# More background steps in the paired projections, the retention gate as a background item, and the gate scan behind three query norms

## The chip, the cores and the metric

One core of a Trainium2 chip. TensorE (PE) multiplies, VectorE (DVE) and ScalarE (ACT) work on elements, GpSimd (POOL) does some element work and issues DMAs, SyncE (SP) issues the other DMAs. The metric is the device time of one execution in microseconds; the median of several runs counts.

## The reference, cut to what matters

Two layers on a sequence of 512 tokens with model width 1024. In each layer the normalized and modulated input h is multiplied by one wide matrix, three attention-like branches are computed from the parts, gated, mixed and added to x; then comes a gated feed-forward part with a short convolution.

```python
h = modulate(rms_norm(x, norm1_g), shift1, scale1)
(rq, rk, rv, rg, gq, gk, gv, glr, gg, fq, fk, fv, ff) = split(h @ w_in)
ret = silu(rg) * head_group_norm(retention(rq, rk, rv))       # branch 0
log_a = log_sigmoid(glr @ w_gla_a2 + b_gla_a) / 16            # the log-decay
gla_o = silu(gg) * rms_norm(gla(gq, gk, gv, log_a))           # branch 1
cum   = cumsum(log_sigmoid(ff + b_fox_f))                     # the scan
fox_o = softmax(rms_norm(fq) @ rms_norm(fk).T + cum_i - cum_j, causal) @ fv   # branch 2
mixed = sum_b sigmoid(h @ w_mg + b_mg)[b] * (branch[b] @ w_br[b]) @ w_o
x = x + gate1 * mixed
h2 = modulate(rms_norm(x, norm2_g), shift2, scale2)
u, g = split(h2 @ w_up)
x = x + gate2 * ((silu(causal_dwconv(u)) * g) @ w_down)
```

The four heads of each branch are 128 wide (gla: keys 64 wide).

## The kernel before, in words

Every weight tile is used in two parts, a high part (`wh`, a cast on ScalarE, line 175) and a low part (`wl`, a subtraction on VectorE, line 184) of the raw tile `wr`; activations likewise (`hhi`, `hlo`). A product takes three matmuls of 512 columns for each 128 x 128 block: high x high, low x high, high x low. A weight unit is 128 x 1024 and is fetched, cast and subtracted a few units ahead. In what follows a "weight matmul" is one of these (lines 295 to 297 in `col_block`, 647 to 651 in the paired projections, 697 to 699 in `tok_group`).

The order in which the program is written is the order on each engine. It is set by hand: the stages of a layer follow each other, and the small work of the branches is put between the weight matmuls in steps. Such small work is a Python generator, an item, in `queue`; `tick()` moves every active item by one step. A step of kind "e" (`E_`) is work of ScalarE, VectorE or GpSimd; a step of kind "p" is TensorE work that takes so many of the three banks of `psa`; a third entry of a step is a condition, and an item whose condition is false stops those behind it too. `cool` counts ticks until the next item may start; every queue entry carries the number for the one behind it, and at most eight are active.

The stages of a layer, with their ticks:

- `head_group`: fq and fk blocks. All eight blocks in layer 0, six in layer 1 (the other two follow in `col_block`s). Behind it the eight `qk_norm` items are queued (square, split into `qsh` and `qsl`, a matmul `qn` of each with ones, then Ln, Exp and squares on ScalarE, a multiply on GpSimd in line 557, two multiplies on VectorE).
- `tok_group`: gk, the log-rank part glr and the forget logits ff, in token order, six ticks; the last two are evacuated into `sml`. `TS` are the sums of h that the paired projections need. Then two `col_block`s for gq. A `col_block` has 24 weight matmuls and two ticks, 12 matmuls apart.
- `pair_group` twice (fv with gv, rv with rg): a matrix product of two halves written as seven products (`prod`) of 24 weight matmuls, each in two halves `t` of 12. Weights are added up in place by DMAs of GpSimd's queue (line 167). A half product has a tick after its sixth matmul if `t < nt`, with `nt` from the list that is given to `pair_group`.
- `col_block`s for rq, rk (rotary) and gg; then three mixing branches in the order fox, ret, gla, each with its gates (`h @ w_mg`) and its product with `w_br`. A branch waits by ticks until its four heads are done. Ahead of the third, ticks are given without weight matmuls until queue and active items are empty: the drain.
- the product with `w_o`, the feed-forward part.

The other items: `gates_item` (transposes `sml` with the matmul `smT`, then |.|, Exp, Ln, the scan `cum`, a matmul `cumc`, and the broadcast of cum by GpSimd's DMAs, lines 748 and 751), `la_item` twice (log-decay), 16 `fox_item`s (`fs`, softmax in `fl`, transposes `fT`, `fpT`, `fo`), four `kv_item`s, 16 `ret_item`s (`rs`, `rP`, `ro`, group norm in `ros`, transposes `oT`), four `gla_item`s (`go`, `gos`, `oT`). `r_done` runs at the end of the second paired projection and makes the retention gate `rg` (tanh on ScalarE in line 997, a multiply on VectorE in line 998, four of each), all in one go.

Of the kernel before, what the change touches and what calls it, by code (L numbers as in the profile page):

```python
# [13 lines left out]
E_ = ("e", 0)  # L14
# [17 lines left out]
NB = S // 128  # L32
# [56 lines left out]
def tile_hybrid_layers(ctx: ExitStack, tc: tile.TileContext, xT, cvec, wall, wada, par, a2, cst, tabs, out):  # L89
# [14 lines left out]
    def slot(nm, dt=F32):  # L104
        return slots.tile([128, S], dt, tag="slot", name=nm)
# [6 lines left out]
    def free(n=1):  # L112
        live[0] -= n

    def ba(nm="ba"):
        live[0] += 1
        return psa.tile([128, S], F32, tag="a", name=nm)
# [3 lines left out]
    def cc(n):  # L121
        o, w = CC[n]
        return C[:, o:o + w]
# [123 lines left out]
    queue = []  # L247
# [38 lines left out]
    cool = [0]  # L286
# [17 lines left out]
    def ahead():  # L304
        prep_to(cur[0] + depth[0])
        dma_to(cur[0] + depth[0] + far[0], far[0] > 1)
# [230 lines left out]
    def layer(l, nm, h):  # L537
        R = {}
# [42 lines left out]
        A.preload_act_table_set("natural_log_exp_and_others")  # L581
        for i, o in enumerate(banks):
            qk_evac(i)(o)
        cool[0] = 12 if l else 8
        ahead()
        free(NA)

# [119 lines left out]
        def gk_evac(b, o):  # L707
            if b == 0:
                R["gk"] = [slot("gk"), slot("gk")]
                R["sml"] = sm_p.tile([128, NB, 20], F32, tag="sml", name="sml")  # L710
            A.copy(R["gk"][b // 2][:, (b % 2) * 256:(b % 2) * 256 + 256], o[:, 0:256])
            V.tensor_copy(R["sml"][:, b, :], o[:, 256:276])
            if b == NB - 1:
                queue[0:0] = [(gates_item(), 2), (la_item(0), 2), (la_item(1), 2)]
                for hh in range(NH):
                    for ib in range(NB):
                        queue.append((fox_item(hh, ib), 1 + ib // 2))

        def gates_item():
            yield P1  # L720
            ps = ba("smT")
            for b in range(NB):
                T.transpose(ps[0:20, b * 128:b * 128 + 128], in_=R["sml"][:, b, :], identity=cc("ident"))
            yield E_
            gl = slot("glrT")
            V.memset(gl[0:32, :], 1.0)
            V.tensor_copy(gl[0:20, :], ps[0:20, :])
            free()
            e = slot("fe")
            m = slot("fm")  # L730
            fb = pp(l, "foxb")[0:4]
            A.activation(e[0:4], gl[0:4], AF.Abs, bias=fb)
            A.activation(e[0:4], e[0:4], AF.Exp, scale=-1.0)
            A.activation(e[0:4], e[0:4], AF.Ln, bias=cc("one")[0:4])
            V.tensor_scalar(m[0:4], gl[0:4], fb, 0.0, op0=ALU.add, op1=ALU.min)
            yield E_
            R["glrT"] = gl
            V.tensor_tensor(m[0:4], m[0:4], e[0:4], op=ALU.subtract)
            V.memset(e[0:4], 1.0)
            cum = slot("cum")  # L740
            V.tensor_tensor_scan(cum[0:4], e[0:4], m[0:4], 0.0, op0=ALU.mult, op1=ALU.add)
            yield P1
            pc = ba("cumc")
            for b in range(NB):
                T.transpose(pc[:, b * 4:b * 4 + 4], in_=cum[0:4, b * 128:b * 128 + 128],
                            identity=cc("ident")[0:4, 0:4])
            cd = dr_p.tile([NH, S], F32, tag="cumd", name="cumd")
            G.dma_start(out=cd, in_=cum[0:NH])
            cb = [slot("cumb") for _ in range(NH)]
            for hh in range(NH):  # L750
                G.dma_start(out=cb[hh], in_=cd[hh:hh + 1, None, :].to_broadcast([1, 128, S]))
            yield E_
            R["cumc"] = sm_p.tile([128, 16], F32, tag="cumc", name="cumc")
            V.tensor_copy(R["cumc"], pc[:, 0:16])
            free()
            R["cumb"] = cb
# [5 lines left out]
        def la_item(bp):  # L762
            yield ("p", 1, lambda: ["glrT" in R])
            ps = ba("la")
            for j in range(2):
                b = 2 * bp + j
                T.matmul(ps[:, j * 256:j * 256 + 256], lhsT=R["glrT"][0:21, b * 128:b * 128 + 128], rhs=a2t[l],
                         start=True, stop=True)
            yield E_
            e, la = slot("lae"), slot("la")  # L770
            A.activation(e, ps, AF.Abs)
            A.activation(e, e, AF.Exp, scale=-1.0)
            A.activation(e, e, AF.Ln, bias=cc("one"))
            V.tensor_scalar(la, ps, 0.0, None, op0=ALU.min)
            free()
            yield E_
            V.tensor_tensor(la, la, e, op=ALU.subtract)
            yield P2
            pS, pa = ba("laS"), ba("lan")
            for j in range(2):  # L780
                T.matmul(pS[:, j * 256:j * 256 + 256], lhsT=cc("suf"), rhs=la[:, j * 256:j * 256 + 256],
                         start=True, stop=True)
            for p in range(2):
                for j in range(2):
                    o = p * 4 + j * 2
                    T.matmul(pa[:, o:o + 2], lhsT=la[:, j * 256 + p * 128:j * 256 + p * 128 + 128], rhs=cc("ind"),
                             start=True, stop=True)
            yield E_
            A.activation(e, pS, AF.Exp, scale=1.0 / 16.0)
            an = sm_p.tile([128, 8], F32, tag=f"an{bp}", name="an")  # L790
            A.activation(an, pa[:, 0:8], AF.Exp, scale=1.0 / 16.0)
            R["an"][bp] = an
            free(2)
            yield E_
            V.tensor_tensor(e, e, R["gk"][bp], op=ALU.mult)
            R["kd"][bp] = e
# [141 lines left out]
        def ret_item(hh, jb):  # L938
            w = S - jb * 128
            yield ("p", 1, lambda: [("rq", hh) in R, ("rk", hh) in R, ("rv", NB - 1) in R, ("dec", hh) in R])  # L940
            ps = ba("rs")
            T.matmul(ps[:, 0:w], lhsT=R["rk", hh][:, jb * 128:jb * 128 + 128], rhs=R["rq", hh][:, jb * 128:S],  # L942
                     start=True, stop=True)
            yield E_
            pt = slot("rP")
            V.tensor_tensor(pt[:, 0:w], ps[:, 0:w], R["dec", hh][:, 0:w], op=ALU.mult)
            R["rP", hh, jb] = pt
            free()
            yield P0 if jb else P1
            if jb == 0:  # L950
                R["ro", hh] = ba("ro")
            po = R["ro", hh]
            for j in range(jb + 1):
                T.matmul(po[:, jb * 128:jb * 128 + 128],  # L954
                         lhsT=R["rP", hh, j][:, (jb - j) * 128:(jb - j) * 128 + 128],
                         rhs=R["rv", j][:, hh * 128:hh * 128 + 128], start=j == 0, stop=j == jb)
            if jb < NB - 1:
                return
            yield E_
            os, dump = slot("ros"), slot("rsq")  # L960
            st = sm_p.tile([128, 12], F32, tag="rst", bufs=4, name="rst")
            for b in range(NB):
                A.activation(os[:, b * 128:b * 128 + 128], po[:, b * 128:b * 128 + 128], AF.Identity,
                             accum_out=st[:, b:b + 1])
            free()
            yield E_
            V.tensor_scalar(st[:, 0:4], st[:, 0:4], -1.0 / HD, None, op0=ALU.mult)
            for b in range(NB):
                A.activation(dump[:, b * 128:b * 128 + 128], os[:, b * 128:b * 128 + 128], AF.Square,
                             bias=st[:, b:b + 1], accum_out=st[:, 4 + b:5 + b])  # L970
            yield E_
            V.tensor_scalar(st[:, 4:8], st[:, 4:8], 1.0 / HD, EPS, op0=ALU.mult, op1=ALU.add)
            G.tensor_tensor(st[:, 8:12], st[:, 4:8], cc("mhalf").to_broadcast([128, 4]), op=ALU.pow)
            yield from head_out(0, hh, os, st[:, 8:12], st[:, 0:4], der[l][:, 24 + hh:25 + hh], R["rg"])

        for i in range(len(banks), 8):
# [14 lines left out]
                    queue.append((kv_item(p, half), 1))  # L991

        def r_done(v, g):
            R["rg"] = []
            for b in range(NB):
                t = slot("rg")
                A.activation(t, g[b], AF.Tanh, scale=0.5)
                V.scalar_tensor_tensor(out=t, in0=t, scalar=1.0, in1=g[b], op0=ALU.add, op1=ALU.mult)
                R["rv", b] = v[b]
                R["rg"].append(t)  # L1000

        pair_group(fg_done, [1] * 7)
        R["cos"], R["sin"] = slot("cos"), slot("sin")
        Q.dma_start(out=R["cos"], in_=tabs[0])
        Q.dma_start(out=R["sin"], in_=tabs[1])
        pair_group(r_done, [1] * 4 + [2] * 3)
        tt.clear()
        far[0] = 1
        for i in range(4):
# [390 lines left out]
```

## Time and profile before

| | |
|---|---|
| median of three runs | 1847.52 us (1846.37 to 1849.38) |
| the profiled execution | 1847.6 us |
| its span, first to last instruction | 1845.8 us |
| mean granted TensorE clock | 0.989 |
| TensorE matmuls busy | 1796.4 us, 97% |
| VectorE busy | 1067.9 us, 58% |
| ScalarE busy | 727.9 us, 39% |
| GpSimd busy | 125.7 us, 7% |
| HBM | 131 GB/s over the span |

Rows of the profile are read so: "L549 PE MATMUL qn<-qsh,onesr" is line 549 of the kernel, engine TensorE, output tile qn, inputs qsh and onesr. In a timeline the first two numbers are the start in us from the span's start and the duration; matmul durations overlap, so the step between starts tells the pace. In square brackets stands how long the engine was idle ahead of the instruction and what released it. In a table of groups "x16 | 11.0, 686 | 0.1" is count, busy us, mean ns of one, and idle us before them. A table by stretches has the stretch, its length, busy us and count of PE, weight loads, VectorE, ScalarE and GpSimd, then the granted clock, the DMA share and GB/s. [...]

### The profile page before, as it was taken

What the parts mean: (1) busy time and instruction counts of PE and PEld (TensorE: products, weight loads), DVE (VectorE), ACT (ScalarE), POOL (GpSimd) and SP (SyncE); (2) the same over time, 40 slices, a digit from 0 to 9 for tenths busy, and PEclk for the clock granted to TensorE, in tenths of its full rate; (3) what the DMA queues carried; (4) which work ended last, traced back from release to release, by engine and by line L of the source; (5) the groups of instructions that cost most, each with busy time, mean ns of one, the idle gap of its engine ahead of it and who ended that gap; (6) DMA issues with size and microseconds to landing.
All of it is one profiled execution on the core that took longest, in us unless ns stands there. A gap on an engine that the chain in (4) does not pass through costs nothing.

```text
span 1845.8 us, 22722 instructions
## 1 busy us (share of the span) xinstructions
PE 1796.4 (97%) x8895; PEld 1493.8 (81%) x8895; DVE 1067.9 (58%) x1643; ACT 727.9 (39%) x1200; POOL 125.7 (7%) x152
## 2 busy tenths in 40 slices
PE   9999899989999999999999989999899999999999
PEld 6877677868889888888897867788688898888887
DVE  7867765576665777663257577644534466444321
ACT  3567543342333433332135684423423244333220
POOL 3122110010000000000001111000100000000000
PEclk9999999989999999999999999999899999999999
DMA  9487134336552465554224861322232233223131
GB/s 358 123 202 194 46 119 133 126 109 224 181 183 81 160 228 183 196 199 141 97 75 124 209 182 34 127 80 69 76 128 94 69 104 113 93 92 103 40 128 50
DMA packets 72519, 243.11 MB, mean 132 GB/s; under 512 B 8232, under 2 KB 8658, under 8 KB 72412
## 3 DMA queue, kind: packets, MB, share of 16 engines
q1 hardware_dynamic: 66444, 220.67, 35.5%
q0 software_dynamic: 5968, 20.99, 5.8%
q8 instruction: 70, 1.15, 0.2%
q14 instruction: 37, 0.30, 0.1%
HBM read 237.41 MB, written 4.21 MB: 131 GB/s over the span
## 4 chain that ended last, share of the span: by engine, by line
PE 83%; DVE 8%; ACT 5%; issue 2%; DMA 1%; POOL 0%; SPq 0%; ACTq 0%; DVEq 0%; POOLq 0%
PE bm L295 22%; PE bm L297 22%; PE bm L296 21%; PE bm L428 4%; PE ga L428 4%; ACT wh L175 2%; DVE wl L184 2%; PE bm L649 2%; PE bm L647 2%; PE bm L651 2%; PE rs L942 1%; PE ro L954 1%; DVE fl L809 1%; DMA wr<-wall 1%; DVE rt L841 1%
## 5 line engine op out<-in xcount | busy, mean ns | idle before, releaser
L184 DVE TENSOR_TENSOR wl<-wr,wh 128x1024 fp32r<-128x1024 f32 x326 | 399.0, 1228 | 299.1 <-ACT wh L175 298.8
L295 PE MATMUL bm<-hhi,wh 128*128 128x512 f32 x1232 | 498.5, 405 | 0.0
L297 PE MATMUL bm<-hhi,wl 128*128 128x512 f32 x1232 | 481.5, 391 | 0.0
L296 PE MATMUL bm<-hlo,wh 128*128 128x512 f32 x1232 | 481.0, 390 | 0.0
L175 ACT CAST wh<-wr 128x1024 fp32r<-128x1024 f32 x326 | 339.0, 1046 | 338.7 <-PE bm L296 235.0
L295 PEld LDWEIGHTS bm<-hhi,wh 128*128 128x128 f32 x1232 | 232.3, 189 | 52.4 <-issue 4.7
L296 PEld LDWEIGHTS bm<-hlo,wh 128*128 128x128 f32 x1232 | 232.4, 189 | 51.4 <-issue 3.3
L297 PEld LDWEIGHTS bm<-hhi,wl 128*128 128x128 f32 x1232 | 231.9, 188 | 49.8
L295 PE MATMUL bm<-fah,wh 128*128 128x512 f32 (+1 forms) x374 | 141.0, 377 | 0.0
L297 PE MATMUL bm<-fah,wl 128*128 128x512 f32 (+1 forms) x374 | 140.8, 377 | 0.0
L296 PE MATMUL bm<-fal,wh 128*128 128x512 f32 (+1 forms) x374 | 140.8, 377 | 0.0
L205 DVE SCALAR_TENSOR_TENSOR ar<-ar,cact 128x1024 f32<-128x1024 f32 x80 | 97.4, 1218 | 0.0
L1083 DVE SCALAR_TENSOR_TENSOR x<-bm,mod,x 128x512 f32<-128x512 f32 (+1 forms) x39 | 25.5, 654 | 101.5 <-PE bm L297 101.5
L297 PEld LDWEIGHTS bm<-fah,wl 128*128 128x128 f32 x374 | 70.4, 188 | 12.9
L295 PEld LDWEIGHTS bm<-fah,wh 128*128 128x128 f32 x374 | 70.4, 188 | 12.9
L296 PEld LDWEIGHTS bm<-fal,wh 128*128 128x128 f32 x374 | 70.4, 188 | 12.9
L1120 ACT ACTIVATE fu<-fu 128x512 f32<-128x512 f32 x44 | 27.8, 632 | 102.5 <-DVE fu L1118 102.5
L1121 DVE TENSOR_TENSOR fu<-fu,bm 128x512 f32<-128x512 f32 x42 | 28.9, 688 | 64.9 <-PE bm L297 53.5
L334 ACT ACTIVATE sq<-x 128x512 f32<-128x512 f32 (+1 forms) x35 | 18.8, 545 | 103.9 <-DVE x L1083 102.9
L295 PE MATMUL bm<-mxh,wh 128*128 128x256 f32 (+1 forms) x176 | 58.6, 333 | 0.0
L297 PE MATMUL bm<-mxh,wl 128*128 128x256 f32 (+1 forms) x176 | 58.3, 331 | 0.0
L296 PE MATMUL bm<-mxl,wh 128*128 128x256 f32 (+1 forms) x176 | 58.3, 331 | 0.0
(258 smaller groups left out, 2716.9 us busy)
## 6 DMA issues: line engine op xcount, KB each, us to landing
wr<-wall SPq DMA_DIRECT2D x302, 512.0 KB, 3.4
ar<-wada SPq DMA_DIRECT2D x80, 512.0 KB, 3.4
wr<-wall POOLq DMA_DIRECT2D x32, 512.0 KB, 7.6
ad<-wada SPq DMA_DIRECT2D x32, 256.0 KB, 6.1
x<-xT SPq DMA_DIRECT2D x16, 256.0 KB, 4.8
cumb<-cumd POOLq DMA_DIRECT2D x8, 256.0 KB, 4.3
dec<-tabs SPq DMA_DIRECT2D x8, 256.0 KB, 2.7
x<-xs SPq DMA_DIRECT2D x8, 256.0 KB, 5.6
```

Source lines behind the costliest of these rows:

```text
L175: A.copy(hi, raw[plan[i][1]])
L184: V.tensor_tensor(lo, raw[plan[i][1]], hi.bitcast(F32), op=ALU.subtract)
L205: V.scalar_tensor_tensor(out=r, in0=r, scalar=1.0, in1=cact, op0=ALU.mult, op1=ALU.mult, accum_out=mod[l][:, b:b + 1])
L295: T.matmul(o, lhsT=wh, rhs=ah, start=first, stop=False)
L296: T.matmul(o, lhsT=wh, rhs=al, start=False, stop=False)
L297: T.matmul(o, lhsT=wl, rhs=ah, start=False, stop=last)
L428: T.matmul(banks[f % GB][:, ts], lhsT=got[f // 8][wi][:, (f % 8) * 128:(f % 8) * 128 + 128], rhs=h[kc][hi][:, ts], start=kc == 0 and hf != ...
L647: T.matmul(banks[t], lhsT=ah[:, ts], rhs=wh[:, ws], start=first and k == 0, stop=False, skip_group_check=True)
L649: T.matmul(banks[t], lhsT=ah[:, ts], rhs=wl[:, ws], start=False, stop=False, skip_group_check=True)
L651: T.matmul(banks[t], lhsT=al[:, ts], rhs=wh[:, ws], start=False, stop=k == 3, skip_group_check=True)
L1120: A.activation(t, t, AF.Silu)
L1121: V.tensor_tensor(t, t, pg, op=ALU.mult)
```

## The change

Four edits in one diff. Every half product of both paired projections has a tick (`[2] * 7`). `cool` starts two ticks lower, and the gates and log-decay items are put three places back in the queue instead of at its front. The retention gate is made by an item (`rg_item`), put at the front of the queue when the second paired projection ends, in one step for each tanh and each multiply. A `ret_item` waits for the four gate tiles before it applies them.

```diff
-        cool[0] = 12 if l else 8
+        cool[0] = 10 if l else 6
...
-                queue[0:0] = [(gates_item(), 2), (la_item(0), 2), (la_item(1), 2)]
+                queue[3:3] = [(gates_item(), 2), (la_item(0), 2), (la_item(1), 2)]
...
             G.tensor_tensor(st[:, 8:12], st[:, 4:8], cc("mhalf").to_broadcast([128, 4]), op=ALU.pow)
+            yield ("e", 0, lambda: [len(R["rg"]) == NB])
             yield from head_out(0, hh, os, st[:, 8:12], st[:, 0:4], der[l][:, 24 + hh:25 + hh], R["rg"])
...
         def r_done(v, g):
+            for b in range(NB):
+                R["rv", b] = v[b]
+            queue.insert(0, (rg_item(g), 1))
+
+        def rg_item(g):
             R["rg"] = []
             for b in range(NB):
+                yield E_
                 t = slot("rg")
                 A.activation(t, g[b], AF.Tanh, scale=0.5)
+                yield E_
                 V.scalar_tensor_tensor(out=t, in0=t, scalar=1.0, in1=g[b], op0=ALU.add, op1=ALU.mult)
-                R["rv", b] = v[b]
                 R["rg"].append(t)
 
-        pair_group(fg_done, [1] * 7)
+        pair_group(fg_done, [2] * 7)
...
-        pair_group(r_done, [1] * 4 + [2] * 3)
+        pair_group(r_done, [2] * 7)
```

Line numbers behind line 973 grow by one to seven: the gate's tanh and multiply are lines 1004 and 1006 afterwards.

The number of instructions is the same on PE, DVE, POOL and SP; ACT has eight table loads fewer. How they move, at three places (the same in both layers; the rows are those of layer 0):

TensorE at the end of the queue, before: the drain ahead of the third branch, between the gate matmuls (hhi) and the branch product (obh).

```order
L297 MATMUL bm<-hhi,wl 128x512
L903 MATMUL oT<-cst,ros 128x128 x4
L954 MATMUL ro<-pr,rP 128x128 x4
L920 MATMUL go<-st,gq 64x128 x8
L903 MATMUL oT<-cst,gos 128x128 x4
L920 MATMUL go<-st,gq 64x128 x8
L903 MATMUL oT<-cst,ros 128x128 x4
L903 MATMUL oT<-cst,gos 128x128 x4
L920 MATMUL go<-st,gq 64x128 x8
L295 MATMUL bm<-obh,wh 128x512
```

TensorE now, one of the places over which the same work is spread, all of them between weight matmuls:

```order
L297 MATMUL bm<-hhi,wl 128x512
L903 MATMUL oT<-cst,ros 128x128 x4
L903 MATMUL oT<-cst,gos 128x128 x4
L920 MATMUL go<-st,gq 64x128 x8
L295 MATMUL bm<-hhi,wh 128x512
```

The last background matmul of the layer now stands 36 weight matmuls ahead of the place where the drain was; before, two transposes came behind it.

ScalarE at the end of the second paired projection, before: the gate in one go, then the last two norms (L553 to L556, qsh).

```order
L675 ACTIVATE pr<-bm 128x512
L997 ACT_TABLE_LOAD
L997 ACTIVATE rg<-pr 128x512 x4
L553 ACT_TABLE_LOAD
L553 ACTIVATE qy<-qn,cst 128x512
L554 ACTIVATE qv<-qn,cst 128x512
L555 ACT_TABLE_LOAD
L555 ACTIVATE qy<-qy 128x512
L556 ACTIVATE qsq<-qy 128x512
L530 CAST qsh<-qsq 128x512
```

ScalarE now: the gate's tanh between softmax steps (fl, fpT) of the fox items.

```order
L822 COPY fpT<-fT 128x384
L815 ACTIVATE fl<-fl,fst 128x512
L1004 ACT_TABLE_LOAD
L1004 ACTIVATE rg<-pr 128x512
L175 CAST wh<-wr 128x1024
L822 COPY fpT<-fT 128x512
L1004 ACTIVATE rg<-pr 128x512
L812 ACTIVATE fl,fst<-fl,fst 128x128
```

The norms are all done by then, and each has its Ln and Exp without a table load.

GpSimd's queue from the first weight sum of the layer, before: weight sums (L167), the cum broadcast, weight sums, and norm multiplies (L557) late.

```order
L167 DMA wr<-wall 128x1024 x3
L748 DMA cumd<-cum 4x512
L751 DMA cumb<-cumd 128x1x512 x4
L167 DMA wr<-wall 128x1024 x7
L557 TENSOR_TENSOR qsq<-qsq,qv 128x512
L167 DMA wr<-wall 128x1024 x4
L557 TENSOR_TENSOR qsq<-qsq,qv 128x512
```

GpSimd's queue now: four norm multiplies come among the first weight sums, and the cum broadcast behind them.

```order
L167 DMA wr<-wall 128x1024 x3
L557 TENSOR_TENSOR qsq<-qsq,qv 128x512 x2
L167 DMA wr<-wall 128x1024 x3
L557 TENSOR_TENSOR qsq<-qsq,qv 128x512
L167 DMA wr<-wall 128x1024
L557 TENSOR_TENSOR qsq<-qsq,qv 128x512
L167 DMA wr<-wall 128x1024
L748 DMA cumd<-cum 4x512
L751 DMA cumb<-cumd 128x1x512 x4
```

The first four norms thus run in the token, gq and first paired stages, 24, 18 and 24 weight matmuls apart, ahead of `smT`; the last four follow the log-decay 24 apart, where they were 24 to 48 apart before.

## The prediction

> **What bounds the kernel now.** I read the page's busy times first, then what TensorE (PE) waited for, then the timeline around the longest waits, and the granted clock there.
>
> ```profile
> span 1845.8 us, 22722 instructions
> PE 1796.4 (97%) x8895; PEld 1493.8 (81%) x8895; DVE 1067.9 (58%) x1643; ACT 727.9 (39%) x1200; POOL 125.7 (7%) x152
> ```
>
> TensorE is the bound: 97% busy. Only its remaining 49 us of idle time can be won, and what runs slowly because of that idle time. The waits of PE, with total, count and longest:
>
> ```profile
> PE oT L903 <- DVE gos L896: 6.6, 4, 2.1
> PE oT L903 <- DVE ros L899: 5.4, 2, 3.0
> PE cumc L745 <- DVE cum L741: 4.1, 2, 2.1
> PE smT L723 <- DVE sml L712: 2.2, 1, 2.2
> ```
>
> The oT rows are the transposes of the last heads. All fall in one place per layer, where the third branch may not start until the queue of background items is empty, and the steps follow each other with no weight matmul between them:
>
> ```profile
> 383.31 0.39 PE L297 MATMUL bm<-hhi,wl 128*128 128x512 f32 x1
> ...
> 399.58 0.79 PE L295 MATMUL bm<-obh,wh 128*128 128x512 f32 x1
> ...
> 404.37 0.39 PE L297 MATMUL bm<-obh,wl 128*128 128x512 f32 x1
> 404.60 0.40 PE L295 MATMUL bm<-obh,wh 128*128 128x512 f32 x1
> ...
> 1296.31 0.60 PE L903 MATMUL oT<-cst,ros 128*128 128x128 f32 x4
> 1296.75 1.06 PE L954 MATMUL ro<-pr,rP 128*128 128x128 f32 x8
> 1297.73 1.09 PE L920 MATMUL go<-st,gq 64*64 64x128 f32 x16
> ...
> 1311.22 0.79 PE L295 MATMUL bm<-obh,wh 128*128 128x512 f32 x1
> ...
> 1315.64 0.39 PE L296 MATMUL bm<-obl,wh 128*128 128x512 f32 x1
> ```
>
> A weight matmul starts every 0.23 us at full clock (404.37 to 404.60). After the drain, eleven starts take 4.79 us (399.58 to 404.37): nearly half speed. The granted clock (third column from the end) says why, also after the shorter wait for cum in the second layer:
>
> ```profile
> 390.00:404.00 14.00, 9.31 (x36) 6.46 (x35) 12.45 (x32) 6.10 (x21) 4.71 (x3) 0.52 0.32 101
> 1007.00:1012.00 5.00, 4.42 (x15) 3.54 (x16) 3.57 (x6) 3.18 (x5) 2.34 (x5) 0.66 0.06 21
> ```
>
> So a long idle stretch is paid twice, once as idle and once at a clock of about a half behind it.
>
> **The change part by part.**
>
> *The drain goes (both layers).* A second step per product in two groups of seven gives 7 more steps in the first group and 4 in the second; the queue then ends, by the order, 36 weight matmuls before the third branch. In the drain stand four oT (0.44 us each, start to start), one ro and three go (0.98 each, by the rows 1296.75 and 1297.73): 5.7 us of work that stays, between matmuls. Layer 0: 399.58 − 383.54 − 5.7 = 10.3 us, and 4.79 − 11 × 0.23 = 2.3 at the low clock. Layer 1: 1311.22 − 1296.31 − 5.7 = 9.2, and 4.42 − 10 × 0.23 = 2.1. Together **−24.0**. DVE and ACT work of the last heads then lies beside weight matmuls; without that cover the 12.0 us of the oT rows would return.
>
> *The gate burst goes.* At present the end of the second group puts a table load, four tanh and the return loads in front of the last two query/key norms:
>
> ```profile
> 187.07 2.19 ACT L997 ACTIVATE rg<-pr 128x512 f32<-128x512 f32 x4
> L553 ACT ACT_TABLE_LOAD x4 | 5.1, 1283 | 0.1
> 195.00 0.49 PE L549 MATMUL qn<-qsh,onesr 128*128 128x512 f32 x1 [3.78 <-ACT qsh L530]
> 196.40 0.80 PE L550 MATMUL qn<-qsl,onesr 128*128 128x512 f32 x1 [0.90 <-DVE qsl L531]
> 197.28 0.77 PE L295 MATMUL bm<-hhi,wh 128*128 128x512 f32 x1
> ...
> 199.52 0.40 PE L297 MATMUL bm<-hhi,wl 128*128 128x512 f32 x1
> ...
> 1107.73 0.80 PE L549 MATMUL qn<-qsh,onesr 128*128 128x512 f32 x1 [3.78 <-ACT qsh L530]
> 1109.12 0.79 PE L550 MATMUL qn<-qsl,onesr 128*128 128x512 f32 x1 [0.60 <-DVE qsl L531]
> 1110.00 0.77 PE L295 MATMUL bm<-hhi,wh 128*128 128x512 f32 x1
> ...
> 1114.33 0.40 PE L296 MATMUL bm<-hlo,wh 128*128 128x512 f32 x1
> ```
>
> Afterwards all eight norms stand before the gate (order), so its burst delays none of them. Layer 0: 3.78 + 0.90, and 2.24 − 5 × 0.23 = 1.1 at the low clock; layer 1: 3.78 + 0.60 and 4.33 − 10 × 0.23 = 2.0. Together **−12.2**. The gate's work remains: one table load per layer (1.28) now falls among the softmax steps of ACT. Its price on PE lies between nothing and 1.28 a layer; the softmax chain has little slack, so I take it whole: **+2.6**. The wait that the gate adds before the group norm of the first retention head holds nobody: by the order rg is made over 200 weight matmuls (46 us) earlier.
>
> [...]
>
> *Scan and log-decay behind the norms.* The wait for sml (2.2) goes, since sml is long ready: **−2.2**. From smT to cumc PE has 36 weight matmuls where it had 30, 1.4 us more, but DVE and ACT also hold norm work by then; of 4.1 us I leave half (ends: none and all): **−2.05**. The low clock behind it in layer 1 costs 5 × (1 − 0.66) = **−1.7**.
>
> *The norms come twice as densely.* One norm on ACT is the sum of six rows, 3.87 us, and splits on DVE in 1.15:
>
> ```profile
> L553 ACT ACTIVATE qy<-qn,cst 128x512 f32<-128x512 f32 x16 | 11.0, 686 | 0.1
> L554 ACT ACTIVATE qv<-qn,cst 128x512 f32<-128x512 f32 x16 | 10.9, 684 | 2.6 <-PE bm L649 2.6
> L556 ACT ACTIVATE qsq<-qy 128x512 f32<-128x512 f32 x16 | 10.1, 632 | 0.5
> L555 ACT ACTIVATE qy<-qy 128x512 f32<-128x512 f32 x16 | 10.1, 631 | 0.0
> L544 ACT ACTIVATE qsq<-qk 128x512 f32<-128x512 f32 x16 | 10.1, 628 | 0.9 <-DVE qy L560 0.9
> L530 ACT CAST qsh<-qsq 128x512 fp32r<-128x512 f32 x16 | 9.7, 605 | 0.0
> L531 DVE TENSOR_TENSOR qsl<-qsq,qsh 128x512 fp32r<-128x512 f32 x16 | 18.3, 1146 | 30.7 <-ACT qsh L530 21.1 <-POOL qsq L557 9.6
> L175 ACT CAST wh<-wr 128x1024 fp32r<-128x1024 f32 x326 | 339.0, 1046 | 338.7 <-PE bm L296 235.0 <-issue 54.6 <-DMA wr<-wall 32.8
> ```
>
> By the order, ACT issues three norms, four weight casts and eleven shorter copies between the first and the fourth norm's matmuls: 3 × 3.87 + 4 × 1.05 = 15.8 us without the copies. PE has 66 weight matmuls there, 15.2 us, and three pairs of norm matmuls. ACT becomes the bound of that stretch. For later norms at this density the trace has a row: the last products already take two steps, and there PE waits
>
> ```profile
> 162.91 0.50 PE L647 MATMUL bm<-wh,tbh 128*128 128x512 f32 x1 [0.69 <-ACT pr L669]
> 171.11 0.50 PE L550 MATMUL qn<-qsl,onesr 128*128 128x512 f32 x1 [0.42 <-DVE qsl L531]
> 185.26 0.50 PE L550 MATMUL qn<-qsl,onesr 128*128 128x512 f32 x1 [0.21 <-DVE qsl L531]
> ```
>
> that is 1.3 us for three to four norms, 0.37 each. A norm's wait lies between 0.37 and the 3.78 above. The last four of a layer are like those rows: 1.5 a layer. The first four stand on the token sums: in layer 0, where DVE was already 2.2 us late with sml and the split queues ahead of sml, I take 6.5 (1.6 each); in layer 1, where nothing waited for sml, 3.5. Less what they replace, 2 × 1.3: 3.0 + 6.5 + 3.5 − 2.6 = **+10.4**.
>
> *GpSimd's queue.* The weight sums (L167, DMAs) of the first group now stand behind four norm multiplies, each of which waits for ACT; before, they stood behind the cum broadcasts. Their lateness is seen once in ACT:
>
> ```profile
> 109.82 1.05 ACT L175 CAST wh<-wr 128x1024 fp32r<-128x1024 f32 x1 [2.63 <-DMA wr<-wall]
> ```
>
> ACT had slack then and has none now. Nothing to 2.6 a layer on PE; half: **+2.6**. The sums of the second group are issued six units ahead; I cost them at nothing under that cover.
>
> *A low clock behind new waits.* Layer 0's first norm waits near 3.3 us by the above; the nearest rows give 1.1 (behind 3.78) and 1.7 (behind 2.1), so a new wait of that length costs nothing to 1.7. One event, whole: **+1.7**.
>
> [...]
>
> Sum: −24.0 − 12.2 − 2.2 − 2.05 − 1.7 + 2.6 + 10.4 + 2.6 + 1.7 = −24.9 us. The profiled execution took 1847.6 us (span 1845.8 and 1.8 around it), as the median of 1847.52: **1822.7 us**.
>
> **The rivals.**
> - *The new density is free.* All sixteen norms at 0.37 (10.4 → 3.3), no DMA wait, no gate price, no clock event, cum wait gone: 16 us less, 1806. For it: the 0.21 to 0.42 rows. Against it: the ACT count for the first four.
> - *The clock falls again and again.* Each of the first four norms of both layers brings a low-clock stretch at 1.7: 8 × 1.7 − 1.7 = +12, 1835. For it: the row at 1007. Against it: where ACT bounds a stretch, a slower PE loses little.
> - *Slower: weight sums late.* The 32 sums feed 16 half-width products. If POOL's in-order queue holds each product up by the 2.63 of the row, that is 42 us, less the 2.6 already in: 1862. It decides from 1.7 us a product on (24.9 + 2.6 over 16). For it: in-order waits on ACT ahead of DMAs. Against it: the sums are issued three products early, and only three short waits were seen.
> - *No change.* Steps get ahead in the order but their chains (softmax, bank release) move the waits elsewhere, one for one: 1847. Against it: the drain had no matmul to hide behind, every other place has twelve.
>
> **How the numbers follow.** Forecast 0.60 (its own range 1812 to 1832), free 0.15, clock 0.12, no change 0.05, slower 0.08. A change of 0.2%, 3.7 us, is about the least that can be told here. Faster is 0.60 + 0.15 + 0.12 = 0.87, same 0.05, slower 0.08. The range 1806 to 1838 takes in the free case, the clock case with a little more, and leaves out the last two and some edges, 2 in 10.
>
> **What would show it.** Right: no oT wait and full clock before the third branch; four table loads fewer per layer and no 3.78 wait at the norms; norm waits in the token and first pair group instead, some 8 us in layer 0 and 5 in layer 1. Wrong: ACT waiting for DMA wr in several products, a granted clock under 0.99 overall, or softmax waits (fs, fT) that grow by more than 3 us a layer.

## The result and the profile after

The changed kernel takes 1829.36 us, the median of four runs (1827.52 to 1831.71), beside 1847.1 for the kernel before on the same chip (1846.37 to 1849.38): a ratio of 0.9903, 95% interval 0.9885 to 0.992, or 17.7 us less. The forecast was 1822.7, with a range of 1806 to 1838: the sign came true, most of the mechanism, and seven tenths of the size.

The page of the changed kernel, and what TensorE waited for in the stretches that changed (total, count, longest, in us):

```profile
span 1825.8 us, 22697 instructions
PE 1786.8 (98%) x8895; PEld 1486.4 (81%) x8895; DVE 1059.9 (58%) x1643; ACT 715.8 (39%) x1192; POOL 128.4 (7%) x152
```

```profile
PE qn L550 <- DVE qsl L531: 9.1, 11, 1.1
PE qn L549 <- ACT qsh L530: 5.2, 8, 1.9
PE fs L803 <- DVE fl L807: 4.3, 4, 1.2
PE cumc L745 <- DVE cum L741: 4.0, 2, 2.0
PE fs L803 <- ACT fpT L822: 3.7, 4, 1.0
PE fT L819 <- ACT fpT L822: 2.3, 2, 1.2
...
PE fT L819 <- ACT fl L815: 1.3, 2, 0.6
```

No oT row is left (12.0 us before), and none for smT (2.2). The norms (qn) now wait 14.3 us where they waited 10.7; the waits for cum are as long as ever; the softmax waits (fs and fT) add up to 11.6 where they were 8.2.

The spans of the two profiled executions differ by 20.0 us. Of these 1.6 us (20.02 against 18.45) were gained ahead of the first weight matmul, where the program was not changed. Counted by weight matmuls, layer 0 up to the product with `w_o` gained 9.4 us, the same stretch of layer 1 gained 9.1, and the rest of the program nothing (409.55 and 409.54 us from there to layer 1, 411.80 and 411.79 from there to the end). So 18.5 us are the change's own.

At the place of the drain, TensorE's timeline now shows the last heads' work between weight matmuls, and the third branch's first product behind its gates without a break (the profile counts each `go` matmul twice, so x16 is one item's eight):

```profile
367.08 0.60 PE L903 MATMUL oT<-cst,ros 128*128 128x128 f32 x4
367.51 0.60 PE L903 MATMUL oT<-cst,gos 128*128 128x128 f32 x4
368.04 1.09 PE L920 MATMUL go<-st,gq 64*64 64x128 f32 x16
369.06 0.50 PE L295 MATMUL bm<-hhi,wh 128*128 128x512 f32 x1
...
391.70 0.39 PE L297 MATMUL bm<-hhi,wl 128*128 128x512 f32 x1
391.93 0.39 PE L295 MATMUL bm<-obh,wh 128*128 128x512 f32 x1
...
397.37 0.39 PE L295 MATMUL bm<-hhi,wh 128*128 128x512 f32 x1
```

From 391.70 to 397.37 are 25 weight matmuls in 5.7 us, 0.23 each. Before, the same 25 took 24.0 (383.31 to 407.34), with the drain among them.

At the first norms the waits are there that the forecast put there:

```profile
82.07 0.49 PE L549 MATMUL qn<-qsh,onesr 128*128 128x512 f32 x1 [1.90 <-ACT qsh L530]
83.41 0.50 PE L550 MATMUL qn<-qsl,onesr 128*128 128x512 f32 x1 [0.84 <-DVE qsl L531]
```

### The profile page after: what moved, and what is told of

It reads as the page before. It is cut to its first block, busy times and chain, and to the rows that moved or that the text cites. A ratio compares the mean times of both kernels' runs of the same rounds, so it can differ in the third digit from the quotient of the medians.

```text
span 1825.8 us, 22697 instructions
## 1 busy us (share of the span) xinstructions
PE 1786.8 (98%) x8895; PEld 1486.4 (81%) x8895; DVE 1059.9 (58%) x1643; ACT 715.8 (39%) x1192; POOL 128.4 (7%) x152
## 4 chain that ended last, share of the span: by engine, by line
PE 83%; DVE 8%; ACT 5%; issue 2%; POOL 1%; DMA 0%; SPq 0%; POOLq 0%; ACTq 0%; DVEq 0%
PE bm L295 22%; PE bm L297 22%; PE bm L296 22%; PE bm L428 4%; PE ga L428 4%; DVE wl L184 2%; ACT wh L175 2%; PE bm L647 1%; PE bm L651 1%; PE bm L649 1%; PE ro L954 1%; PE rs L942 1%; DVE fl L809 1%; DVE qsl L531 1%; POOL qsq L557 1%
## 5 line engine op out<-in xcount | busy, mean ns | idle before, releaser
L1090 DVE SCALAR_TENSOR_TENSOR x<-bm,mod,x 128x512 f32<-128x512 f32 (+1 forms) x39 | 25.5, 655 | 101.5 <-PE bm L297 101.5
L296 PEld LDWEIGHTS bm<-fal,wh 128*128 128x128 f32 x374 | 70.4, 188 | 12.7
L1050 ACT ACTIVATE mg<-bm,der 128x512 f32<-128x512 f32 x48 | 33.0, 688 | 65.2 <-PE bm L297 65.2
```

The costliest lines, as they stand in the source:

```text
L296: T.matmul(o, lhsT=wh, rhs=al, start=False, stop=False)
L1050: A.activation(g, o, AF.Tanh, scale=0.5, bias=der[l][:, i * 8 + j:i * 8 + j + 1])
L1090: V.scalar_tensor_tensor(out=x[j][:, ts], in0=o[:, ts], scalar=mod[l][:, sec * 8 + j:sec * 8 + j + 1], in1=x[j][:, ts], op0=ALU.mult, op1= ...
```

## The experiments

A ratio is always to the runs of the kernel before on the same chip, whose median lay between 1846.2 and 1848.7. Two things were not tried: doubled steps with nothing else changed, and the early split without doubled steps.

| run | what differs from the changed kernel | median, us | ratio (95%) |
|---|---|---|---|
| the changed kernel | | 1829.4 | 0.9903 (0.9885 to 0.992) |
| 1 | gate in one go | 1830.8 | 0.9904 (0.9888 to 0.9919) |
| 2 | old steps | 1834.5 | 0.9924 (0.9908 to 0.9939) |
| 3 | the norm's split a step earlier | 1821.9 | 0.9857 (0.9841 to 0.9873) |
| 4 | a step behind the scan | 1822.6 | 0.9858 (0.9839 to 0.9877) |
| 5 | 3 and 4 together | 1812.0 | 0.9815 (0.98 to 0.9829) |
| 6 | old steps, gate in one go (new place of the scan alone) | 1832.3 | 0.9927 (0.991 to 0.9943) |
| 7 | old steps, old place of the scan (gate item alone) | 1834.2 | 0.9935 (0.992 to 0.995) |
| 8 | scan at the front of the queue | 1832.0 | 0.9922 (0.9907 to 0.9937) |
| 9 | the norm's multiply on DVE | 1826.5 | 0.9887 (0.9872 to 0.9902) |
| 10 | 3, 4 and 9 together | 1814.4 | 0.9824 (0.981 to 0.9839) |
| 11 | 3 and 4, gate in one go | 1812.0 | 0.9806 (0.979 to 0.9823) |

**1: the gate in one go, the rest as changed.**

```diff
-            yield ("e", 0, lambda: [len(R["rg"]) == NB])
...
         def r_done(v, g):
-            for b in range(NB):
-                R["rv", b] = v[b]
-            queue.insert(0, (rg_item(g), 1))
-
-        def rg_item(g):
             R["rg"] = []
             for b in range(NB):
-                yield E_
...
-                yield E_
...
+                R["rv", b] = v[b]
```

> The changed kernel with the gate made in one go again (steps and order as changed). By the order the eight norms still stand ahead of the gate and the drain is still gone. Theory A (the density of steps and the order carry the gain; the gate item only spreads 3.5 us of ScalarE work per layer): slower than the changed kernel by 0 to 4 us a layer, so 1830 to 1837 us, no wait of a norm for qsh over 2 us, fs or fT waits larger by up to 3.5 us a layer. Theory B (the gate item itself removes the burst's 12.2 us): about 1841 us, with waits of 3.8 us behind the gate.

The ratio is that of the changed kernel: beside doubled steps the item is worth nothing that can be told (theory A). What the burst (the four tanh in one go) delays now is not a norm but the evacuation of a gate product, in this run's waits of TensorE:

```profile
PE bm L295 <- ACT mg L1043: 3.6, 2, 1.8
```

and the changed kernel waits 2.0 us more for softmax copies (the row fs from fpT is 3.7 there, 1.7 here).

**2: the old steps, with the gate item and the new place.**

```diff
-        pair_group(fg_done, [2] * 7)
+        pair_group(fg_done, [1] * 7)
...
-        pair_group(r_done, [2] * 7)
+        pair_group(r_done, [1] * 4 + [2] * 3)
```

> The changed kernel with the old numbers of steps in both paired projections (gate item and order as changed). By the order 16 transposes stand in the drain again. Theory A (the extra steps empty the queue before the third branch, worth 24 us, and cost about 11 us in norm waits): near 1829 + 24 - 6 = 1847 us, with half clock behind the drain. Theory B (the order and the gate item carry most of the gain): about 1835 us.

1834.5: theory A's 1847 missed by far, and B's value is right. The drain is back, with its clock (0.5 for 13.7 us from 383.5 and for 10.2 from 1291.5; over the whole run the granted clock is 0.990, 0.996 in the changed kernel). But other waits left with the steps; in this run TensorE waits

```profile
PE oT L903 <- DVE ros L899: 7.4, 2, 4.0
PE qn L550 <- DVE qsl L531: 5.5, 10, 0.9
PE fT L819 <- ACT fl L815: 5.0, 2, 2.5
PE qn L549 <- ACT qsh L530: 3.5, 3, 1.9
```

with no row for cum at all, and 9.0 at the norms instead of 14.3. Added up over the two stretches that changed, TensorE is idle for 31.1 us with the old steps and 30.4 with the new. The doubled steps removed a drain and gave nearly all of its idle time back at the norms, at cum and in the softmax; over the two stretches the profiled executions differ by 5.0 us, and what idle time does not account for lies in the clock (34.2 us at half clock there, 10.2 in the changed kernel) and in small matmuls that no longer run at half speed (in the kernel before, the eight `go` of an item take 1.97 us at half clock and 1.09 at full). The intervals of the two ratios overlap, so by the runs alone the worth of the doubled steps beside the other edits is not shown.

**6 and 7: one edit at a time.** Number 6 keeps of the change only the new place of the scan and the earlier start, number 7 only the gate item.

```diff
 6:
-                queue[0:0] = [(gates_item(), 2), (la_item(0), 2), (la_item(1), 2)]
+                queue[3:3] = [(gates_item(), 2), (la_item(0), 2), (la_item(1), 2)]
 7:
+            queue.insert(0, (rg_item(g), 1))
```

> Only the new place of scan and log-decay (three places back, start two ticks earlier); old steps and the gate in one go. Order and gate item together gave -14 (1834.5). Theory A, they are separate: the order takes the sml wait (2.2), both cum waits (4.1) and the low clock behind one of them (1.7), and costs some 1 to 2 us of norm waits: -6 to -7, 1841; the 3.78 waits at the norms behind the gate stay. Rival B, the order makes the whole of -14, since earlier norms no longer meet the gate's burst: 1834 to 1836, no 3.78 waits.

> Only the gate as a background item; old steps and old place of the scan. Theory A: the waits behind the burst go (3.78 twice, and 0.6 to 0.9, and the low clock behind them 3.1: 12.2 in all), the load among the softmax steps costs 2.5 in each layer as it did with the order: -7, 1841. Rival B: the burst's work only moves on to the softmax, one for one: 1846 to 1848. With steps doubled the item was worth nothing (1830.8 without it); A puts that down to the norms, which the steps already bring ahead of the gate.

Both missed theory A, which had them near 1841 each. By the medians the new place alone saves 13.9 us and the gate item alone 12.0, but both together (number 2) only 14.2. Either is enough to take the 3.78 waits away: the earlier start brings the last norm in front of the burst, the item brings the burst behind the last norm.

The two differ at the drain. For the same 25 weight matmuls as above, which took 24.0 us in layer 0 and 22.8 in layer 1 before, number 6 takes 16.0 and 15.5, number 7 takes 27.1 and 25.5, and number 2, which is number 6 with the gate item, 22.0 and 21.2. So the earlier start shortens the drain without any doubled step: with the weight matmuls (5.7) and the small work taken off (5.7 before, 3.3 in number 6) it cost 12.7 and 11.4 us before and costs 7.0 and 6.6 here, so that some 10 of the 13.9 us are won there. The gate item lengthens the queue and gives most of this back. That, beside the shared cure of the 3.78 waits, is why the two savings don't add.

Where the 3.78 waits were, a wait of the softmax remains. Number 6, TensorE around the end of the second group in layer 0:

```profile
183.82 0.39 PE L549 MATMUL qn<-qsh,onesr 128*128 128x512 f32 x1
...
197.71 0.47 PE L819 MATMUL fT<-cst,fl 128*128 128x128 f32 x1 [3.19 <-ACT fl L815]
```

Number 7 has the last norm there without any wait, and shorter waits of the softmax behind it (total, count, longest); the waits for cum, ahead of the norms, are as before (4.1).

```profile
PE fT L819 <- ACT fl L815: 5.3, 4, 1.7
```

**3: the split of the norm's squares a step earlier.** It is the same number of steps, with the split in the square's step.

```diff
             A.activation(sq, raw_t, AF.Square)
-            yield E_
             sh, sl = split(sq, "qs")
+            yield E_
             yield P1
```

> The changed kernel with the split of a norm's square (qsh, qsl) issued one step earlier, in the step of the square, so that 24 weight matmuls instead of 12 lie between it and the norm's matmul; the number of steps and of instructions is the same. Theory A (the norm waits of 14.2 us are the latency of the ScalarE-VectorE chain against 12 matmuls): norm waits fall under 5 us and two stretches at half clock go, about 1816 us. Theory B (ScalarE is out of throughput there): the waits stay within 3 us of 14 or move to the evacuations, 1826 to 1830 us.

The norm waits fell from 14.3 to 2.5 us, so a longer lead was enough; ACT, which does exactly the same work, was not full. That is theory A in kind. In size it missed: 1821.9, a gain of 7.5 where 13 was written. Part came back in other places, first at cum (4.0 before this edit). The norms' two rows and the new waits:

```profile
PE cumc L745 <- DVE cum L741: 6.2, 2, 3.2
...
PE la L767 <- ACT qsq L556: 2.8, 2, 1.4
...
PE ba L647 <- ACT qv L554: 2.1, 2, 1.0
PE bm L295 <- DVE sml L712: 1.7, 2, 1.1
...
PE qn L550 <- DVE qsl L531: 1.4, 3, 0.6
...
PE qn L549 <- ACT qsh L530: 1.1, 1, 1.1
```

**4: a step between the scan and the matmul that transposes it.**

```diff
             V.tensor_tensor_scan(cum[0:4], e[0:4], m[0:4], 0.0, op0=ALU.mult, op1=ALU.add)
+            yield E_
             yield P1
```

> The changed kernel with one empty step between the scan and the matmul of cum (12 weight matmuls, 2.7 us more). Theory A (the 2.0 us wait for cum, twice, is a distance too short by less than one step, and brings a stretch at half clock in layer 0): cum waits gone, 4.0 + 1.7 us less, 1823 to 1825 us. Theory B (what is saved is lost in the log-decay steps behind, which are later): within 1.5 us of the changed kernel's 1829.4.

The cum waits are gone, 4.0 us, and the norm waits stay (8.7 and 5.9). The time fell by 6.8, a little more than A's 4 to 6.

**5: both.**

```diff
-            yield E_
             sh, sl = split(sq, "qs")
+            yield E_
...
             V.tensor_tensor_scan(cum[0:4], e[0:4], m[0:4], 0.0, op0=ALU.mult, op1=ALU.add)
+            yield E_
```

> The early split and the step behind the scan together (each alone, against the changed kernel's 1829.4: -7.5 and -6.8). Theory A, the two waits are separate latencies: the early split's cum waits (6.2 us, two) go as they went with the scan step alone, the norm waits stay at 2.5, so the gains add: about -14, 1815. Rival B, ACT is full in the stretch behind the token sums and what one chain wins another loses (the early split had new waits for the log-decay, 4.9, and for sml, 1.7): those grow to 8 or more and the time stays at 1820 to 1822. A time under 1817 speaks for A.

1812.0: theory A, the gains add. By the medians, which come from different chips, it is 3 us better than the sum; by the ratios the sum would be 0.9812, and 0.9815 was measured. The waits of TensorE in this run, those that the two edits were to move:

```profile
PE la L768 <- ACT qsq L556: 2.7, 2, 1.4
PE bm L295 <- DVE sml L712: 1.7, 2, 1.1
PE qn L550 <- DVE qsl L531: 1.4, 3, 0.6
PE qn L549 <- ACT qsh L530: 1.1, 1, 1.1
PE cumc L746 <- DVE cum L741: 0.4, 1, 0.4
```

Between the half-clock stretches at the very start and end of the execution a single one of 3.4 us is left, of three. This version is 34 us faster than the kernel before, about twice what the change brought.

**8: the scan at the front of the queue again, with doubled steps.**

```diff
-                queue[3:3] = [(gates_item(), 2), (la_item(0), 2), (la_item(1), 2)]
+                queue[0:0] = [(gates_item(), 2), (la_item(0), 2), (la_item(1), 2)]
```

> The changed kernel with scan and log-decay at the front of the queue again (steps, earlier start and gate item as changed). Theory A, with doubled steps the place is worth little: the sml wait comes back (2.2 in layer 0), the cum waits stay or grow by 1, the first norms wait less (-3): 1827 to 1831. Rival B, the place is worth with doubled steps what it is worth alone (6 to 7): 1835 to 1837, with the sml wait, cum waits and a low clock behind them.

1832.0 lies between the theories, a little nearer to A's upper end, and its interval overlaps that of the changed kernel: beside doubled steps no value of the place alone is shown. The wait for sml did not come back, against both theories; the waits for cum (5.3) and for the split (12.7) are longer.

**9 and 10: the norm's multiply on DVE.**

```diff
-            G.tensor_tensor(t, t, v, op=ALU.mult)
+            V.tensor_tensor(t, t, v, op=ALU.mult)
```

> The changed kernel with the norm's multiply (L557) on DVE instead of GpSimd. In the changed kernel the DVE split before the norm matmul takes 1.36 us where that multiply runs on GpSimd at the same time, and 0.68 otherwise; 9.1 us of waits stand on it. Theory A, the two engines slow each other down: multiply 0.68 and then split 0.68 on DVE end about 0.55 earlier than the 1.36 now, so the waits on the split fall from 9.1 to some 4, the time by 3 to 5: 1825. Rival B, the split's lateness is ACT's (its cast stands behind four activations of the norm before): the waits stay at 9 or more, and 1829 or, with 0.7 us more work per norm on DVE, 1832.

> Early split and scan step (1812.0) and the norm's multiply on DVE as well. With the early split the split already takes 0.68 and its waits are down to 1.4 us. Theory A (the engines' contention is what the early split took away): nothing left to win, 1811 to 1813. Rival B (contention elsewhere, in the weight splits of DVE beside GpSimd, costs PE time too): 1808 or less. Slower than 1815 would say that DVE's own queue is now the late one.

The group of the DVE split (nanoseconds: shortest, median, longest), in the changed kernel, in number 9 and in number 3:

```profile
L531 DVE TENSOR_TENSOR qsl<-qsq,qsh x16: 681/1360/1780, 82.7 to 1061.1; 128x512 fp32r<-128x512 f32 x16
```

```profile
L531 DVE TENSOR_TENSOR qsl<-qsq,qsh x16: 683/685/692, 84.7 to 1061.2; 128x512 fp32r<-128x512 f32 x16
```

```profile
L531 DVE TENSOR_TENSOR qsl<-qsq,qsh x16: 681/684/693, 81.1 to 1050.2; 128x512 fp32r<-128x512 f32 x16
```

With no multiply on GpSimd the split never takes more than 0.69 us, and the waits on it fall from 9.1 to 5.2. That is theory A's mechanism, and 1826.5 is close to its 1825; but the intervals of the ratios overlap, so the gain isn't shown, and the log-decay matmul has a new wait:

```profile
PE la L767 <- issue: 3.9, 2, 2.0
```

Number 3 shortens the split just as much by moving it out of the multiply's time, so its gain has two parts that were not separated further: at most about 4 of its 11.8 us of norm waits come from splits that are slower beside the multiply, by number 9 (9.1 to 5.2). Number 10 says that nothing more is to be had: 1814.4 beside 1812.0, with overlapping intervals.

**11: both latency edits, the gate in one go.** It differs from number 5 by the edit of number 1.

```diff
         def r_done(v, g):
-            for b in range(NB):
-                R["rv", b] = v[b]
-            queue.insert(0, (rg_item(g), 1))
-
-        def rg_item(g):
             R["rg"] = []
```

> Early split and scan step (1812.0), but the gate made in one go. Alone the item was worth 12, beside the doubled steps 1.4 with overlapping intervals. Theory A, the item only matters while a norm stands behind the gate: as all norms are still earlier here, 1811 to 1815. Rival B, with the other waits gone ACT's burst at the end of the second group is seen in the softmax and in the gates (waits for mg, 3.6 before): 1817 to 1820.

1812.0, the same as with the item: theory A again. Once steps are doubled, the gate item can be left out without a loss that can be told.

## Why the prediction was right, and where it was off

- *Drain, −24.0.* Right: 24.0 us became 5.7 in layer 0 and 23.7 became 6.6 in layer 1 for the same weight matmuls, less 5.7 of work that moved in each: −24.0 (18.4 − 5.7 and 17.1 − 5.7). Measured against the kernel before the term holds. Number 2 qualifies it: removing the drain by steps paid only as far as the steps' new waits were smaller. And the prediction put the drain's end down to the steps alone, while number 6 took 10.5 us off its cost in the two layers with the old steps.
- *Gate burst, −12.2.* The 3.78 waits and those behind them are gone. Numbers 6 and 7 show that two edits of the change each take them away, and number 1 that the gate item is not needed for it: the prediction, which credited the order, was right there.
- *Gate's load and GpSimd's queue, +2.6 and +2.6.* The softmax waits grew by 3.4 us, and a wait of 1.1 for the log-decay (`ba`) went. ACT waits for weights by DMA in fewer places (six, 26.1 us, where it was ten and 32.8), so the late weight sums did not occur; this is why the slower rival failed. The two together came to 3.4 − 1.1 = 2.3 instead of 5.2.
- *sml, −2.2.* Gone, as said.
- *cum, −2.05, and the low clock behind it, −1.7.* The step that failed. Six more weight matmuls of lead (36 for 30) bought nothing: 2.0 us in each layer as before. DVE's timeline says why, the reason that the prediction named and then gave half the weight:

```profile
113.01 0.69 DVE L560 SCALAR_TENSOR_TENSOR qy<-qsq,qy 128x512 f32<-128x512 f32 x1 [1.18 <-POOL qsq L557]
113.73 0.75 DVE L562 SCALAR_TENSOR_TENSOR qk<-qk,der,qy 128x512 f32<-128x512 f32 x1
114.40 0.67 DVE L738 TENSOR_TENSOR fm<-fm,fe 4x512 f32<-4x512 f32 x1
115.24 0.48 DVE L739 MEMSET fe<- 4x512 f32 x1 [0.16 <-DVE fm L738]
115.75 1.21 DVE L741 TENSOR_TENSOR_SCAN cum<-fe,fm 4x512 f32<-4x512 f32 x1
```

  A norm's last multiplies, themselves waiting for GpSimd, now stand on DVE ahead of the scan. The extra step of number 4 (48 weight matmuls of lead) takes the wait away, and numbers 2 and 6, where the old steps leave 72 at the new place, have none: the doubled steps took back most of the lead that the new place gave. The low clock left layer 1 and appeared in layer 0 (below), so that term came out at 0.
- *Norms, +10.4.* Net +11.3 (14.3 now; 10.7 and 1.4 before, of which 9.1 is the burst's). The shares were off: 4.9 and 3.7 us at the first four norms (6.5 and 3.5 forecast), 2.8 in each layer at the last four (1.5 forecast). The reason given, ACT as the bound of that stretch, was wrong. Around the fourth norm (its cast is the second row), ACT stands idle twice and waits for TensorE:

```profile
98.83 0.59 ACT L657 COPY pr<-bm 128x512 f32<-128x512 f32 x1 [1.43 <-PE bm L651]
102.62 0.60 ACT L530 CAST qsh<-qsq 128x512 fp32r<-128x512 f32 x1
107.09 0.59 ACT L658 COPY pr<-bm 128x512 f32<-128x512 f32 x1 [2.44 <-PE bm L651]
```

```profile
103.25 1.36 DVE L531 TENSOR_TENSOR qsl<-qsq,qsh 128x512 fp32r<-128x512 f32 x1 [2.75 <-ACT qsh L530]
```

```profile
103.27 0.49 PE L549 MATMUL qn<-qsh,onesr 128*128 128x512 f32 x1 [0.39 <-ACT qsh L530]
104.67 0.50 PE L550 MATMUL qn<-qsl,onesr 128*128 128x512 f32 x1 [0.90 <-DVE qsl L531]
```

  The wait is latency: cast, then split, then matmul, all within one step, with the cast behind the activations of the norm before. Number 3 shows it, where all engines have the same work and 11.8 of 14.3 us go.
- *Low clock behind new waits, +1.7.* Two events behind norms (84.4 and 995.8 us, 3.4 us each): eight weight matmuls at 0.43 instead of 0.23 each, 3.2 us. The rival of a clock that falls at every norm did not come: 16 norms, 2 falls.
- *Not priced:* weight matmuls right behind small work start slower (0.38 us to the next start, on average, in place of 0.23), and there are more such breaks now, 141 at full clock in place of 131: some 1.3 us more.

With what was measured for each term the sum is near −20.4 where −18.5 was found; about 2 us aren't placed.

## What to carry to other kernels

Here spreading queued work over more slots moved nearly as much idle time as it removed. So count the lead that each chain (cast, split, matmul) has in its new slot: the waits in these slots were latency and not throughput, and one step of lead for the split and one for the scan took 16 to 17 us off, where the doubled steps took 4 to 5, too little for the intervals to tell. When two edits cure the same wait, try them one at a time: here place and gate item brought 13.9 and 12.0 us alone and 14.2 together, and the place alone had shortened the drain that the steps were meant for. A wait of 2.07 us for cum in the kernel before cost nothing more in layer 0, and in layer 1 another 1.6 us behind it, at a granted clock of 0.50 for 3.41 us (eight weight matmuls at 0.43 in place of 0.23 each).

## What the runs showed of the hardware

*Stretches at half clock.* In the kernel before they start 196.04, 390.60, 1008.41, 1107.40, 1301.96 and 1844.68 us behind the first instruction, in the changed kernel 12.75, 84.43, 118.56, 995.78 and 1825.22. From the first of them to the others that is 57, 238, 267, 324 and 483 times 3.4133 us, and 21, 31, 288 and 531 times (agreeing to 0.01). They last 3.41, 6.83 or 13.65 us, but for the last one of each, with which the execution ends. A 2.0 us wait for cum stands in both layers and before and after, but behind only two of the four is a stretch at half clock. The changed kernel in pieces of 3.41 us, with borders at whole multiples of 3.4133 us from these starts; third column from the end the granted clock, for layer 0 and layer 1; then layer 1 of the kernel before:

```profile
115.15:118.56 3.41, 1.45 (x9) 1.28 (x10) 3.29 (x4) 1.57 (x3) 0.56 (x1) 1.00 0.71 135
118.56:121.97 3.41, 3.41 (x10) 2.18 (x8) 3.41 (x6) 1.53 (x2) 1.22 (x3) 0.50 0.53 162
...
1016.26:1019.68 3.42, 2.73 (x12) 1.88 (x11) 2.56 (x5) 3.39 (x5) 1.41 (x2) 1.00 0.62 101
1019.68:1023.09 3.41, 2.09 (x12) 1.80 (x13) 3.41 (x4) 1.05 (x3) 0.55 (x1) 1.00 0.55 109
1023.09:1026.50 3.41, 3.41 (x15) 2.37 (x14) 3.03 (x5) 1.45 (x2) 2.17 (x4) 1.00 0.71 219
```

```profile
1005.00:1008.41 3.41, 1.34 (x9) 0.85 (x8) 3.21 (x6) 3.35 (x6) 0.55 (x1) 1.00 0.43 84
1008.41:1011.83 3.42, 3.42 (x9) 2.65 (x9) 2.16 (x3) 1.67 (x3) 1.62 (x3) 0.50 0.06 20
```

Where the wait lies whole in one piece, TensorE is busy for 1.45 or 1.34 us of it, and the next piece is at 0.50; the same wait across a border leaves 2.73 and 2.09, and the pieces behind are at 1.00. Idle time alone gives no sharp bound: in the kernel before, half clock follows a piece with 1.29 us idle (from 1298.55) and does not follow one with 1.69 (from 79.99). Counted back in the same steps, the first border lies 1.48 us behind the first instruction in the kernel before and 2.51 in the changed kernel.

*DVE and GpSimd.* A 128x512 DVE split takes 0.68 us. In the changed kernel ten of the sixteen start some 0.5 us after a GpSimd multiply of the same size, and each of these ends 0.55 us after that multiply does: they take 1.36 to 1.41 us beside multiplies of 1.27 to 1.31, and 1.78 beside two of 1.84. Number 9, without a multiply on GpSimd, has 0.69 at most: it is the multiply's doing. How the one slows the other is not shown. Beside a multiply this link of the chain takes twice its time. A split that is issued a step earlier no longer meets the multiply (0.68 to 0.69 in all sixteen of number 3), and taking the multiply off GpSimd then gains nothing that can be told (number 10: 1814.4 beside 1812.0).
